# Two stacked transformer blocks on one core: gate products copied out of PSUM, modulation moved out of the second block's attention, raw context stream in its second layer

## The chip, the cores and the metric

The kernel runs on one core of a Trainium2 chip. The metric is the device time of one execution in microseconds (us), taken as the median of several runs. All arithmetic is float32; a matrix product is written as three matmuls on rounded halves (`hi`, `lo`) of both operands, which TensorE takes in its fp32r format.

## The reference

Two two-layer networks run one after the other on 256 latent tokens of width 1024.

`first_block`: per layer an RMS norm, three attention branches (neighbourhood, latent, windowed grouped-query), gates, an output projection, and a feed-forward net with a short convolution; a last RMS norm with `final_g`.

`second_block` takes that result as `x_lat`, with 256 context tokens `x_ctx` beside it. Cut to what the change touches:

```python
for l in range(DEPTH):
    last = l == DEPTH - 1
    m_lat = modulation(c, w_mod[l], b_mod[l])       # silu(c) @ w_mod + b: 6 vectors of 1024
    m_ctx = modulation(c_ctx, w_mod[l], b_mod[l])
    h_lat = modulate(rmsnorm_2(x_lat, norm1_g[l]), sh1, sc1)
    h_ctx = modulate(rmsnorm_2(x_ctx, norm1_g[l]), csh1, csc1)
    z_lat = h_lat @ w_in[l]                         # q, k, v, u, g
    z_ctx = h_ctx @ w_in[l][:, kv_lo:kv_hi] if last else h_ctx @ w_in[l]
    attn_lat = gqa_blocks(qh_l, concat(kh_c, kh_l), concat(vh_c, v_l))
    gm_lat = gelu(u_l) * spatial_mix(group_layernorm(gelu(g_l)))
    x_lat = x_lat + ga1 * (concat(attn_lat, gm_lat) @ w_out[l])
    x_lat = x_lat + ga2 * sqrelu_mlp(modulate(rmsnorm_2(x_lat, norm2_g[l]), sh2, sc2))
    # not last: the same two updates for x_ctx, with attention over the context alone
```

## The kernel before

Activations lie with features on partitions and tokens on the free axis: `xx` holds the latents in its columns 0 to 255 (`LAT`) and the context in 256 to 511 (`CTX`), as 8 tiles of 128 features. Weights come in pieces of 128 x 2048 by `load_w` (L161): one DMA on SyncE's queue into one of three `raw` buffers, then for each half a ScalarE copy to `hi` (L170) and a VectorE subtraction to `lo` (L172); five `hi` and five `lo` buffers exist. `pin[0]`, when set, keeps those `lo` subtractions behind a named VectorE instruction.

PSUM: four `acc` tiles for products, two `s` tiles for attention scores, one `pt` for transposes, one `o` for attention outputs and small sums. A matmul group waits until VectorE and ScalarE have read the tile that it takes over.

The instructions of each engine are put in order by the framework's scheduler from the order of the code, dependencies and priorities, so an edit can shift neighbours too. In the code, `weave(main, side, ratio)` runs `ratio` steps of a generator `side` per step of `main`.

Modulation: the 6 x 1024 modulation values of both layers and streams are dot products on VectorE (L280), in 192 steps; each step loads 128 x 512 of `w_mod` into one of two `mraw` buffers and makes two reductions of some 0.75 us (one in the last 64 of the steps). Steps 0 to 95 are layer 1, 96 to 191 layer 2. Every `load_w` ends with `tick()`, which adds the current rate to a counter and runs a step for each whole unit; `mod_until(n)` runs what is missing up to step n. `R1[layer]` holds the four rates of a layer of block 1 (start, attention and merge, up projection, down projection), `R2` the three of block 2 (preparation, attention, feed-forward).

Block 2, per layer, in the code's order: the projections of k, v and q (`z_lat`, `z_ctx`); q and k norms and rotation (`q_done`, `k_done`, collected in `prep`); the gate half of the gated unit (`g_half`, GELU and group statistics, `normalise`); then `attn()`, woven with `fill`: the `u` tiles of the gated unit (`gate_tile`, `twice_gelu`), their mixing matmuls (L1129), and the half of the output projection that needs them. The first `PRE[l]` steps of `fill` run ahead of attention. Then come the other half of the output projection, norm and feed-forward in four quarters `qq`, each four pieces up (FF1) and four down (FF2).

A stream can be multiplied in two ways. `mod_rows` makes the normed and modulated tile (L319, L321, L322) before the product. The other way, `raw_shift` and `raw_tile`, splits the unnormed tile times the scale, adds two columns for the shift (so 258 columns, `TE`), and the norm's row factor is applied to the product in `finish` (L898 to L902).

`twice_gelu` computes a GELU by tanh; its `x` is a PSUM tile `acc`, which is read by L1104, L1106 and L1108.

Of the kernel before, what the change touches and what calls it, by code (L numbers as in the profile page):

```python
# [3 lines left out]

# [1 line left out]

# [8 lines left out]
AF = mybir.ActivationFunctionType  # L15
# [6 lines left out]
T = 256  # L22
# [32 lines left out]

WV = (0.34, 1.48, 0.48)

R1 = ((0.0, 1.05, 0, 0.96), (0.23, 1.0, 0, 0.03))

R2 = (1.18, 1.45, 3.23)  # L60
SWAP16 = [i ^ 16 for i in range(32)]


# [12 lines left out]
def program(tc, A, out, stop=None):  # L76
# [10 lines left out]
    with top:  # L87
# [220 lines left out]
        def stream():  # L308

            return Parts([u8([P, 2, 4, TE], F32R) for _ in range(2)])  # L310
# [4 lines left out]
        def mod_rows(pool, bufs, row, a, sh, s, h):  # L315

            for k in range(KD):
                t = mk(pool, [P, T], tag="nt", bufs=bufs)
                V.scalar_tensor_tensor(t, xx[:, k, cut(s)], a[:, k, s : s + 1], row, op0=ALU.mult, op1=ALU.mult)  # L319
                hi, lo = h(k, slice(0, T))  # L320
                S.activation(hi, t, AF.Identity, bias=sh[:, k, s : s + 1])  # L321
                V.scalar_tensor_tensor(lo, t, sh[:, k, s : s + 1], hi.bitcast(F32), op0=ALU.add, op1=ALU.subtract)  # L322
# [8 lines left out]
        def raw_tile(a, s, e, k):  # L331

            return split(xx[:, k, cut(s)], *e(k, slice(0, T)), a[:, k, s : s + 1])
# [526 lines left out]
        def block2():  # L860
            with ExitStack() as st:
# [32 lines left out]
                def mm_x(ps, piece, x, n):  # L894
                    mm_w(ps[:, 0:n], piece, 0, KD, lambda k: x(k, slice(0, n)))
# [9 lines left out]
                for l in range(L):  # L905
# [53 lines left out]

                    def z_ctx(piece, z):  # L960
                        ps = acc()
                        mm_x(ps, piece, hc, T)
                        S.copy(z[:, CTX], ps[:, 0:T])

                    def k_done(kf):
                        rk = head_rms(kf, 4)
# [56 lines left out]
                    if l == 0:  # L1023
                        hc, e, al, wk = glob["start"]
                        row_l = frow[:, 1, :]
                    else:
                        hc = stream()
                        e, row_l, al = lat
                    zs = [tmp() for _ in range(6)]
                    hl = qtab = None  # L1030

# [23 lines left out]
                    else:  # L1055
# [4 lines left out]
                        wq = load_w(A["w_in2"][l, 0], 1024, 2048)  # L1060
                        done()
                        rows_of(rms_cols(tot[1], D), frow[:, 0, :])
                        mod_rows(kp, NT2, frow[:, 0, :], al, sh1, 1, hc)
                        q = u8p()
                        for i in range(2):
                            z_lat(wq[i], zs[2 + i])
# [25 lines left out]
                        next(second)  # L1092
                        next(prep, None)
                    normalise(0)
                    weave(second, prep, 1.0)
                    if l == 0:
                        for k in range(KD):
                            V.scalar_tensor_tensor(xx[:, k, LAT], xx[:, k, LAT], glob["fing"][:, k : k + 1], frow[:, 0, :], op0=ALU.mult, op1=ALU.mult)
                    gm = u8p()

                    def twice_gelu(dst, x, n):

                        th = tmp()[:, :n]
                        S.activation(th, x, AF.Square)  # L1104
                        V.tensor_scalar(th, th, 0.044715 * GC, GC, op0=ALU.mult, op1=ALU.add)
                        V.tensor_mul(th, th, x)  # L1106
                        S.activation(th, th, AF.Tanh)
                        V.scalar_tensor_tensor(dst, th, 1.0, x, op0=ALU.add, op1=ALU.mult)  # L1108

                    def mix_tasks():  # L1110

# [25 lines left out]

                        for g in range(4):
                            yield from gate_tile(g)
                            if g == 0:  # L1140
                                normalise(1)
                            if g:
                                mix(g - 1)
                        mix(3)
# [2 lines left out]
                    def attn():  # L1147
                        hold = {}

                        def front(j, side, b):  # L1150
# [12 lines left out]
                                src = [ps[:, i, :] for i in range(2)]  # L1163
                            s = sc[:, j, bb, :]
                            nm2 = small([P, 2], tag="nm2")
                            ins = V.tensor_mul(nm2, nm, s)
                            if last and (j, side, b) == (0, 0, 0):
                                pin[0] = ins
                            if side == 0:
                                p = [tmp(), tmp()]  # L1170
                            else:
# [38 lines left out]
                    fill = chain(mix_tasks(), out_half(1, gm, gate))  # L1210
                    mod_rate(R2[1])
                    ya = q
                    for _ in range(PRE[l]):
                        next(fill)
                    weave(attn(), fill, WV2[l])

                    def products(ap, x, cols_list, use, first=None):
# [38 lines left out]
                    for qq in range(4):  # L1256
# [19 lines left out]
                        if end and not last:  # L1276
                            mod_until(128)
                            al = scale_of(mods[l + 1], glob["par2"][:, l + 1, 0:8], 1)
                            lat = stream(), frow[:, 2, :], al
                            raw_shift(mods[l + 1][0], 0, lat[0])  # L1280
                            tot = [total_tile() for s in streams]

                        def down(mi, ps, cols):
                            m = 2 * c + mi
                            update(m, ps, 5, cols)
                            if end and last:
                                nc.sync.dma_start(out[:, m, :], xx[:, m, LAT])
                            elif end:
                                for s in range(cols.start // T, cols.stop // T):
                                    if s == 0:  # L1290
                                        raw_tile(al, 0, lat[0], m)
                                    add_square(tot[s], s, m)

                        for c in range(4):
# [138 lines left out]
```

## Time and profile before

| | us |
|---|---|
| median of 3 runs | 1785.15 (1783.11 to 1787.07) |
| the profiled execution, its own time | 1786.61 |
| its span, first to last instruction | 1784.8 |
| TensorE busy in the span | 1750.1 (98%) |
| VectorE busy | 1458.6 (82%) |
| ScalarE busy | 1017.7 (57%) |

Block 1 takes the span up to about 911 us, block 2's first layer from there to about 1471, its second layer the rest. Attention with its fill stands at about 976 to 1085 in the first layer, and at about 1518 to 1590 in the second. A busy share is a mean over stages, and matmuls overlap in the record, so a busy TensorE can still run below its pace; what it waits for is read stage by stage.

### The profile page before, as it was taken

To read this page: it belongs to the slowest core of one execution; us is meant where nothing else is said; L and a number is where in the kernel's file an instruction comes from. 1 tells how busy PE (TensorE), PEld (TensorE's weight loads), DVE (VectorE), ACT (ScalarE), POOL (GpSimd) and SP (SyncE) were. 2 spreads that over 40 slices of the span, in tenths; PEclk is the share of its full clock that TensorE was granted. 3 is DMA by queue.
4 is the path that set the end of the run, shared out by engine and by line. 5 is a ranking of instruction groups with operands and counts; after the bars stand their busy time and mean duration, and the time that the engine had idled before them with its cause. 6 is when DMAs were issued, how large, how long until landed. Compare 5 with 4: busy or idle time off the path is not lost.

```text
span 1784.8 us, 34096 instructions
## 1 busy us (share of the span) xinstructions
PE 1750.1 (98%) x13368; PEld 1673.0 (94%) x13368; DVE 1458.6 (82%) x3176; ACT 1017.7 (57%) x2007; POOL 83.5 (5%) x87
## 2 busy tenths in 40 slices
PE   8999999999999999999999999999999999899999
PEld 8999999999999999999999878989898989799999
DVE  8997899889898788988768878988675768877665
ACT  6866666665585666766554766424251536665453
POOL 0100210000010021000002000000000001000000
PEclk9999999999999999999999999999999999999999
DMA  7364664547645457454543212554545443225552
GB/s 286 127 220 173 208 231 168 187 165 247 212 160 196 171 184 248 168 188 155 189 164 108 90 49 80 179 182 164 178 156 181 145 151 118 94 67 197 187 189 95
DMA packets 69185, 297.11 MB, mean 166 GB/s; under 512 B 7840, under 2 KB 12448, under 8 KB 43424
## 3 DMA queue, kind: packets, MB, share of 16 engines
q1 hardware_dynamic: 68752, 294.67, 47.8%
q8 instruction: 105, 1.72, 0.4%
q14 instruction: 56, 0.46, 0.1%
q10 hardware_dynamic: 272, 0.26, 0.1%
HBM read 293.85 MB, written 1.05 MB: 165 GB/s over the span
## 4 chain that ended last, share of the span: by engine, by line
PE 80%; DVE 11%; ACT 5%; issue 2%; POOL 1%; DMA 0%; POOLq 0%; ACTq 0%; DVEq 0%
PE acc L180 23%; PE acc L182 23%; PE acc L181 23%; DVE lo L172 3%; PE s L180 2%; PE s L181 2%; PE s L182 2%; DVE u L205 1%; PE pt L411 1%; POOL rs_y L218 1%; ACT hi L170 1%; ACT p L386 1%; ACT p L397 1%; PE o L180 1%; DVE mjunk L280 1%
## 5 line engine op out<-in xcount | busy, mean ns | idle before, releaser
L180 PE MATMUL acc<-u,hi 128*128 128x256 f32 (+2 forms) x3604 | 1053.0, 293 | 8.0 <-DVE kf L1108 3.9
L181 PE MATMUL acc<-u,hi 128*128 128x256 f32 (+2 forms) x3604 | 1050.9, 292 | 1.0 <-DVE u L208 0.6
L182 PE MATMUL acc<-u,lo 128*128 128x256 f32 (+2 forms) x3604 | 1047.8, 291 | 1.2 <-DVE lo L172 1.0
L170 ACT CAST hi<-raw 128x1024 fp32r<-128x1024 f32 (+2 forms) x468 | 471.4, 1010 | 436.3 <-PE acc L181 381.0
L180 PEld LDWEIGHTS acc<-u,hi 128*128 128x128 f32 x3604 | 681.9, 189 | 24.9 <-DVE kf L1108 4.3
L181 PEld LDWEIGHTS acc<-u,hi 128*128 128x128 f32 x3604 | 682.8, 189 | 16.2 <-DVE u L208 1.9
L182 PEld LDWEIGHTS acc<-u,lo 128*128 128x128 f32 x3604 | 682.1, 189 | 15.1 <-DVE lo L172 2.1
L172 DVE TENSOR_TENSOR lo<-raw,hi 128x1024 fp32r<-128x1024 f32 (+2 forms) x468 | 551.2, 1184 | 101.7 <-ACT hi L170 95.8
L280 DVE CUSTOM_DVE_ANT_0 mjunk<-mraw,csil,mpart 128x512 bf16<-128x512 f32 x160 | 119.9, 749 | 9.0 <-DMA mraw<-in_w_mod 7.9
L280 DVE CUSTOM_DVE_ANT_0 mjunk<-mraw,csil,c_par 128x512 bf16<-128x512 f32 x160 | 120.2, 751 | 6.3 <-DMA mraw<-in_w_mod 5.2
L1189 DVE SCALAR_TENSOR_TENSOR xx<-acc,mods,xx 128x256 f32<-128x256 f32 x144 | 64.7, 479 | 57.7 <-PE acc L182 57.4
L218 POOL TENSOR_TENSOR rs_y<-rs_v,mhalf 128x2 f32<-128x2 f32 (+2 forms) x29 | 35.2, 1215 | 1080.3 <-DVE rs_v L216 1080.3
L204 ACT CAST u<-nt 128x256 fp32r<-128x256 f32 x146 | 57.2, 405 | 43.2 <-DVE nt L1272 35.0
L902 ACT ACTIVATE nt<-nt,shb 128x256 f32<-128x256 f32 x96 | 48.7, 510 | 57.3 <-DVE nt L901 57.3
L205 DVE TENSOR_TENSOR u<-nt,u 128x256 fp32r<-128x256 f32 x146 | 59.5, 421 | 17.2 <-ACT u L204 15.7
L182 PE MATMUL s<-u,lo 128*128 128x256 f32 x224 | 63.1, 282 | 0.5 <-DVE lo L172 0.5
L180 PE MATMUL s<-u,hi 128*128 128x256 f32 x224 | 62.9, 281 | 0.0
L181 PE MATMUL s<-u,hi 128*128 128x256 f32 x224 | 62.9, 281 | 0.0
L1272 DVE TENSOR_TENSOR nt<-nt 128x256 f32<-128x256 f32 x96 | 40.5, 423 | 19.4 <-ACT nt L902 13.3
L180 PE MATMUL acc<-hi,u 128*128 128x256 f32 (+1 forms) x168 | 48.5, 289 | 0.0
L182 PE MATMUL acc<-hi,u 128*128 128x256 f32 (+1 forms) x168 | 48.2, 287 | 0.0
L181 PE MATMUL acc<-lo,u 128*128 128x256 f32 (+1 forms) x168 | 48.1, 286 | 0.0
(249 smaller groups left out, 2059.2 us busy)
## 6 DMA issues: line engine op xcount, KB each, us to landing
raw<-in_w_ff SPq DMA_DIRECT2D x64, 1024.0 KB, 4.9
raw<-in_w_in SPq DMA_DIRECT2D x61, 1024.0 KB, 4.9
mraw<-in_w_mod SPq DMA_DIRECT2D x192, 256.0 KB, 3.4
raw<-in_w_up SPq DMA_DIRECT2D x44, 1024.0 KB, 4.9
raw<-in_w_down SPq DMA_DIRECT2D x32, 704.0 KB, 4.2
raw<-in_w_out SPq DMA_DIRECT2D x16, 1024.0 KB, 5.0
raw<-in_w_br SPq DMA_DIRECT2D x12, 1024.0 KB, 4.9
nbias<-in_na_bias SPq DMA_DIRECT2D x8, 384.0 KB, 3.0
```

The source lines that it names most:

```text
L170: S.copy(hi[:, : b - a], raw[:, a:b])
L172: last_lo[0] = V.tensor_sub(lo[:, : b - a], raw[:, a:b], hi[:, : b - a].bitcast(F32))
L180: PE.matmul(ps, a[0], b[0], start=start, stop=False)
L181: PE.matmul(ps, a[0], b[1], start=False, stop=False)
L182: return PE.matmul(ps, a[1], b[0], start=False, stop=stop)
L204: S.copy(hi, src)
L205: return V.tensor_sub(lo, src, hi.bitcast(F32))
L218: G.tensor_tensor(y, v, mhalf[:, :n] if len(shape)==2 else mhalf[:, :n].rearrange('p (a b) -> p a b', b=shape[2]), op=ALU.pow)
L280: V.tensor_tensor_reduce(out=junk, in0=w, in1=csil[:, i, half * 512 : half * 512 + 512], op0=ALU.mult, op1=ALU.add, scale=1.0, scalar=part ...
L902: S.activation(dst, dst, func, bias=b)
L1189: V.scalar_tensor_tensor(xx[:, m, cut(s)], ps[:, s * T - cols.start : s * T - cols.start + T], md[i][:, m, s : s + 1], xx[:, m, cut(s)], o ...
L1272: V.tensor_mul(r, r, r)
```

## The change

Eight edits:

1. `R1[1]` goes from (0.23, 1.0, 0, 0.03) to (0.23, 1.25, 0, 0.0), `R2` from (1.18, 1.45, 3.23) to (0, 0, 3.55): no modulation step is tied to a load of block 2's preparation and attention any more; more are in block 1's second attention and in the feed-forward of block 2's first layer.
2. `twice_gelu` copies `x` out of PSUM by ScalarE right behind the square, and the two VectorE instructions read the copy.
3. The context's k and v of the second layer are made from a raw stream. Its tiles are split at the end of the first layer's feed-forward; `mod_rows` for the context goes.
4. The scaling of the latents by `final_g` moves into the fill's third gate tile.
5. The second `normalise` moves from behind the first gate tile to behind the second.
6. The first `PRE[l]` steps of `fill` are woven with what is left of `prep`.
7. The pin on the first maximum of the second layer's attention goes.
8. An import (which moves every line number by one or more).

```diff
-R1 = ((0.0, 1.05, 0, 0.96), (0.23, 1.0, 0, 0.03))
+R1 = ((0.0, 1.05, 0, 0.96), (0.23, 1.25, 0, 0.0))
-R2 = (1.18, 1.45, 3.23)
+R2 = (0.0, 0.0, 3.55)
...
                     def z_ctx(piece, z):
                         ps = acc()
-                        mm_x(ps, piece, hc, T)
-                        S.copy(z[:, CTX], ps[:, 0:T])
+                        if last:
+                            mm_x(ps, piece, hc, TE)
+                            finish(ps, frow[:, 0, :], z[:, CTX], AF.Identity)
+                        else:
+                            mm_x(ps, piece, hc, T)
+                            S.copy(z[:, CTX], ps[:, 0:T])
...
-                        hc = stream()
-                        e, row_l, al = lat
+                        (e, hc), row_l, al = lat
...
                         rows_of(rms_cols(tot[1], D), frow[:, 0, :])
-                        mod_rows(kp, NT2, frow[:, 0, :], al, sh1, 1, hc)
...
                     normalise(0)
-                    weave(second, prep, 1.0)
-                    if l == 0:
-                        for k in range(KD):
-                            V.scalar_tensor_tensor(xx[:, k, LAT], xx[:, k, LAT], glob["fing"][:, k : k + 1], frow[:, 0, :], op0=ALU.mult, op1=ALU.mult)
...
                         S.activation(th, x, AF.Square)
+                        S.copy(dst, x)
                         V.tensor_scalar(th, th, 0.044715 * GC, GC, op0=ALU.mult, op1=ALU.add)
-                        V.tensor_mul(th, th, x)
+                        V.tensor_mul(th, th, dst)
                         S.activation(th, th, AF.Tanh)
-                        V.scalar_tensor_tensor(dst, th, 1.0, x, op0=ALU.add, op1=ALU.mult)
+                        V.scalar_tensor_tensor(dst, th, 1.0, dst, op0=ALU.add, op1=ALU.mult)
...
-                            if g == 0:
+                            if g == 1:
                                 normalise(1)
+                            if g == 2 and l == 0:
+                                for k in range(KD):
+                                    V.scalar_tensor_tensor(xx[:, k, LAT], xx[:, k, LAT], glob["fing"][:, k : k + 1], frow[:, 0, :], op0=ALU.mult, op1=ALU.mult)
...
-                            ins = V.tensor_mul(nm2, nm, s)
-                            if last and (j, side, b) == (0, 0, 0):
-                                pin[0] = ins
+                            V.tensor_mul(nm2, nm, s)
...
-                    for _ in range(PRE[l]):
-                        next(fill)
+                    weave(chain(second, islice(fill, PRE[l])), prep, 1.0)
                     weave(attn(), fill, WV2[l])
...
-                            lat = stream(), frow[:, 2, :], al
-                            raw_shift(mods[l + 1][0], 0, lat[0])
+                            lat = [stream(), stream()], frow[:, 2, :], al
+                            for s in streams:
+                                raw_shift(mods[l + 1][0], s, lat[0][s])
...
-                                    if s == 0:
-                                        raw_tile(al, 0, lat[0], m)
+                                    raw_tile(al, s, lat[0][s], m)
```

VectorE ahead of the first score maximum (L1158, now L1161) of block 2's first attention. `lo` is a weight's second half, `mjunk` a modulation reduction, BN rows are group statistics, `u` is the gate half being normalised. Before:

```order
L172 TENSOR_TENSOR lo_13464<-raw_13457,hi_13463 128x1024
L1008 BN_STATS bn_13103<-u_2241_12748 128x6
L1008 BN_STATS bn_13106<-u_2241_12748 128x6
L1009 BN_AGGR mv_12972<-bn_13103 128x2
L280 ISA mjunk_13470,mpart_13467<-mraw_13468,csil_106,c_par_65_267 128x512
L280 ISA mpart_13467 128x1
L1009 BN_AGGR mv_12972<-bn_13106 128x2
L172 TENSOR_TENSOR lo_13795<-raw_13792,hi_13794 128x1024
L216 TENSOR_SCALAR rs_v_13109<-mv_12972 128x8
L1158 TENSOR_REDUCE nm_13155<-s_13156 128x1
L1158 TENSOR_REDUCE nm_13155<-s_13161 128x1
```

The same place now:

```order
L173 TENSOR_TENSOR lo_13458<-raw_13451,hi_13457 128x1024
L1013 BN_STATS bn_13111<-u_2245_12755 128x6
L1013 BN_STATS bn_13114<-u_2245_12755 128x6
L1014 BN_AGGR mv_12972<-bn_13111 128x2
L1014 BN_AGGR mv_12972<-bn_13114 128x2
L173 TENSOR_TENSOR lo_13792<-raw_13789,hi_13791 128x1024
L217 TENSOR_SCALAR rs_v_13117<-mv_12972 128x8
L1026 TENSOR_SCALAR u_2245_12755<-u_2245_12755,mv_12972,rs_y_13119 128x128 x4
L1161 TENSOR_REDUCE nm_13147<-s_13148 128x1
L1161 TENSOR_REDUCE nm_13147<-s_13153 128x1
L1026 TENSOR_SCALAR u_2245_12755<-u_2245_12755,mv_12972,rs_y_13119 128x128
L1169 TENSOR_TENSOR nm_2311_13158<-nm_13147,sc_12260 128x2
```

The modulation reduction has gone from this stretch; four of the eight normalising instructions of the second half (L1026), which wait for GpSimd's `rs_y`, now stand ahead of the two maxima.

ScalarE at the first two gate tiles of the second layer; L1104 was the square and is now the copy, L1107 is the tanh, `hi` a weight's first half. Before:

```order
L1104 ACTIVATE kf_19286<-acc_19261 128x256
L204 CAST u_3392_18758<-kf_18626 128x256
L170 CAST hi_19795<-raw_19793 128x1024
L204 CAST u_3392_18758<-kf_18627 128x256
L1107 ACTIVATE kf_19286<-kf_19286 128x256
L1104 ACTIVATE kf_19322<-acc_19297 128x256
L1107 ACTIVATE kf_19322<-kf_19322 128x256
```

Now:

```order
L1103 ACTIVATE kf_19275<-acc_19250 128x256
L1104 COPY kf_19249<-acc_19250 128x256
L205 CAST u_3384_18750<-kf_18651 128x256
L171 CAST hi_19797<-raw_19795 128x1024
L1107 ACTIVATE kf_19275<-kf_19275 128x256
L1103 ACTIVATE kf_19317<-acc_19292 128x256
L1104 COPY kf_19291<-acc_19292 128x256
L1107 ACTIVATE kf_19317<-kf_19317 128x256
```

The last reader of each `acc` tile is now ScalarE's copy; the second tile's square and copy still stand behind the first tile's tanh, which waits for VectorE.

## Rows read from the trace of the kernel before

**Rows 1.** The page, busy time of each engine (us, share, instructions).
```profile
PE 1750.1 (98%) x13368; PEld 1673.0 (94%) x13368; DVE 1458.6 (82%) x3176; ACT 1017.7 (57%) x2007; POOL 83.5 (5%) x87
```

**Rows 2.** Busy time by stretch: us, PE PEld DVE ACT POOL, clock, DMA, GB/s.
```profile
484.00:560.00 76.00, 74.91 (x585) 71.62 (x584) 73.39 (x204) 58.89 (x144) 5.57 (x6) 1.00 0.49 170
560.00:715.00 155.00, 154.76 (x1254) 151.15 (x1253) 126.83 (x271) 94.42 (x186) 15.77 (x16) 1.00 0.58 201
976.00:1042.00 66.00, 58.78 (x389) 52.38 (x388) 52.82 (x123) 41.60 (x93) 1.64 (x1) 0.95 0.23 76
1113.00:1159.00 46.00, 45.92 (x359) 44.88 (x360) 45.85 (x117) 23.14 (x54) 0.00 (x0) 1.00 0.54 182
1159.00:1470.00 311.00, 311.00 (x1940) 279.84 (x1939) 230.64 (x514) 111.58 (x224) 0.00 (x0) 1.00 0.49 167
1515.00:1550.00 35.00, 27.92 (x171) 23.82 (x170) 29.68 (x77) 21.50 (x45) 3.08 (x3) 0.90 0.31 115
984.70:988.10 3.40, 3.21 (x9) 2.63 (x10) 3.00 (x13) 2.81 (x7) 0.00 (x0) 0.50 0.16 32
1524.00:1530.80 6.80, 5.24 (x18) 4.56 (x19) 5.27 (x9) 4.67 (x8) 0.00 (x0) 0.50 0.30 104
```

**Rows 3.** Modulation reductions alone (L280), VectorE busy by stretch.
```profile
930.00:976.00 46.00, 6.77 (x18) 1.00 0.27 93
1113.00:1159.00 46.00, 22.63 (x60) 1.00 0.54 182
```

**Rows 4.** TensorE's waits, 930 to 1113 us: releaser, us, times, longest.
```profile
PE s L180 <- ACT kf L386: 4.3, 2, 4.0
PE acc L180 <- DVE kf L1108: 1.8, 1, 1.8
PE o L935 <- DVE rs_v L216: 0.9, 1, 0.9
```

**Rows 5.** TensorE's waits, 1515 to 1600 us.
```profile
PE acc L180 <- DVE kf L1108: 2.1, 1, 2.1
PE acc L1129 <- DVE kf L1108: 2.0, 2, 1.5
PE o L181 <- DVE kf L205: 1.7, 3, 1.0
PE acc L180 <- ACT u L204: 1.3, 1, 1.3
```

**Rows 6.** Timeline, first layer's first scores: start us, us, engine, instruction.
```profile
973.51 1.65 DVE L1098 SCALAR_TENSOR_TENSOR xx<-xx,c_fing,frow 128x256 f32<-128x256 f32 x4
...
976.87 0.40 PE L182 MATMUL s<-kk,u 128*128 128x512 f32 x1
...
981.60 1.29 DVE L1158 TENSOR_REDUCE nm<-s 128x1 f32<-128x512 f32 x2
...
984.89 0.80 PE L180 MATMUL s<-kk,u 128*128 128x512 f32 x1 [4.01 <-ACT kf L386]
```

**Rows 7.** Timeline, one gate tile of the first layer.
```profile
1032.13 0.60 ACT L1104 ACTIVATE kf<-acc 128x512 f32<-128x512 f32 x1
...
1034.65 0.69 DVE L1108 SCALAR_TENSOR_TENSOR kf<-kf,acc 128x512 f32<-128x512 f32 x1 [0.70 <-ACT kf L1107]
...
1035.39 0.51 PE L180 MATMUL acc<-u,hi 128*128 128x512 f32 x1 [1.81 <-DVE kf L1108]
```

**Rows 8.** Groups by line and shape: count | busy us, mean ns | idle before.
```profile
L322 DVE SCALAR_TENSOR_TENSOR u<-nt,mods,u 128x256 fp32r<-128x256 f32 x16 | 6.9, 482 | 0.0
L319 DVE SCALAR_TENSOR_TENSOR nt<-xx,modA,frow 128x256 f32<-128x256 f32 x16 | 6.9, 481 | 1.1 <-ACT frow L228 1.1
...
L204 ACT CAST kf<-pt 128x512 fp32r<-128x512 f32 x24 | 14.0, 582 | 6.0 <-PE pt L411 5.8
L1106 DVE TENSOR_TENSOR kf<-kf,acc 128x512 f32<-128x512 f32 x4 | 2.7, 687 | 0.0
L1135 DVE SCALAR_TENSOR_TENSOR kf<-kf,kf 128x512 f32<-128x512 f32 x4 | 2.7, 685 | 0.1
```

More of the change, by code (lines that the diff above doesn't have):

```diff
@@ L3 @@
 from functools import partial
+from itertools import islice
 import numpy as np
```

## The prediction

> **What bounds the kernel now.** The first view is the page's busy time. TensorE is busy for 98% of the span, VectorE for 82%, ScalarE for 57% [rows 1]. That alone leaves little to gain: 34.7 us of the span without a running matmul. So the second view is busy time by stretch, and there the idle time is not spread. The first 66 us of block 2's first attention hold 7.2 us of it (66.00 less 58.78), and 35 us at the second layer's hold 7.1 us (35.00 less 27.92). The feed-forward behind the first has none in 311 us, and its first 46 us 0.08 us, with VectorE at 45.85 of 46 [rows 2]. A full VectorE is thus no cost by itself: it costs only where a matmul waits for its last word.
>
> The third view, TensorE's waits, says for what. In the first layer 4.3 us go to scores waiting for an exponential (`s` from `kf` L386) and 1.8 us to a product waiting until a gate tile has left PSUM (`acc` from L1108) [rows 4]; in the second, 2.1 and 2.0 us to the same gate tiles [rows 5]. After the long waits the granted clock falls to half (1.2 of 2.4 GHz). Two such windows are shown, 3.4 us and 6.8 us long at 0.50 [rows 2]; there are four in the two attentions, the other two of 3.4 us. A matmul then takes twice its time, so half of the busy time in a window is lost: 1.6 us in the first, 2.6 us in the long one, and 1.7 us in each of the others, where TensorE was busy throughout.
>
> **The change part by part.** The sum is made against the profiled execution's own 1786.6 us, 1.5 us above the median of the runs.
>
> *First scores of the first layer.* The scores are complete at 977.27 us (976.87 plus 0.40), but VectorE takes their maxima at 981.60, 4.3 us late, and the third score tile waits 4.01 us [rows 6]. VectorE is behind with modulation: nine reductions (18 instructions, each reduction having a small read beside it) take 6.77 us just before [rows 3]. In the changed order, between the latents' modulated rows and this maximum, I count 2 reductions where there were 11; nine times 0.75 us is 6.8 us less in front of the maximum, more than it was late. The scaling by `final_g` (1.65 us for four of its eight instructions in rows 6) does not leave the stretch, though the code moves it: the scheduler still puts it in front. What is late next: four normalising instructions now stand ahead of the maxima and wait for GpSimd. I leave 0.9 us for that. Of 4.0 + 1.6 = 5.6 us this gives back 4.7.
>
> *Gate products, first layer.* L1104 starts at 1032.13; the tile is let go when L1108 ends at 1035.34, and the next product, ready 1.81 us before 1035.39, starts then [rows 7]. With the copy, it is let go after the square and one ScalarE copy of 512 columns. The nearest row for that copy is a ScalarE cast of 512 columns out of PSUM, 582 ns [rows 8]: 1032.13 + 0.60 + 0.58 = 1033.31, before the product is ready at 1033.58. So the wait and its clock window go, 1.8 + 1.7 = 3.5 us; I take 3.2.
>
> *Gate products, second layer.* Waits of 2.1 and 2.0 us and 2.6 us of the long window, 6.7 us together. Here the second tile's square and copy stand on ScalarE behind the first tile's tanh, which waits for VectorE, so part of the second wait can stay. I take 5.2. Dropping the pin lets two weight subtractions run before the first maximum; VectorE has 3 us less to do there all the same (below).
>
> *The price of the copies.* Eight on ScalarE, at most 8 x 0.58 = 4.7 us, in stretches where it is busy 41.6 of 66 and 21.5 of 35 us [rows 2]. Behind each in its queue are exponentials and the casts of transposed scores, for which TensorE waits; the cost lies between 0 and 4.7 us, and I take 0.4, near the low end because ScalarE idles over a third of the time. [...] Here the ScalarE cast of 512 columns is shorter (582 ns) than VectorE's product of the same size (687 ns) [rows 8], so the row speaks for ScalarE. [...] The Trainium skill (Perfetto Trace Analysis, Optimizing Scalar/DVE Operations) also gives VectorE about 65 ns more per instruction on PSUM than on SBUF, which would make the 16 rerouted products 1.0 us cheaper; L1106 on PSUM takes 687 ns and L1135 on SBUF 685, so I count nothing.
>
> *Modulation moved.* By the order, 144 reductions stood before block 1's second up projection and 158 do now: 14 x 0.75 = 10.5 us more VectorE work in its attention and merge. In 484 to 560 VectorE has 2.6 us free, in 560 to 715 it has 28 us [rows 2]; one of the 14 falls in the first of these, the rest later. Below nothing it cannot be; above, all 10.5 us could come through; I take 0.5. Each pair of reductions brings a load on SyncE's queue in front of a weight load; three `raw` buffers cover it. In the first layer's feed-forward there are 160 reductions where there were 144, 12 us more, over 357 us in which VectorE has 80 us free: nothing, except in the first quarter, which is a rival below. Outside the two attentions, 0.9 us of waiting for VectorE in the preparation [rows 4] should go by about half: 0.5 us.
>
> *Raw context stream.* Gone: 16 VectorE instructions of 0.48 us [rows 8], 7.7 us, and 8 on ScalarE. Added: eight splits at the end of the feed-forward, about half of that, and two finishes. TensorE takes two columns more in 48 matmuls, 0.1 us. The work gone was beside running matmuls, so it gives nothing itself; it makes VectorE about 3 us earlier at the second layer's first maximum, which the gate term counts on.
>
> *New order.* The scheduler's order changes throughout both attentions. Some new gap will appear between transposes and outputs; I set 1.0 us, between the 1.7 us that such waits (`o` from `kf` L205) took in the second layer [rows 5] and none.
>
> Sum: -4.7 - 3.2 - 5.2 - 0.5 + 0.4 + 0.5 + 0.1 + 1.0 = -11.6. That is 1775.0 by the profiled execution and 1773.5 by the median; I predict 1774 us, with 1771 to 1777 as the likeliest case's own range.
>
> **The rivals.** *The attention's own chain takes over.* In the second layer's new order 36 matmuls of the fill stand between the first and second pair of scores, where 14 did; they are missing later, where a round of transpose, cast, subtraction and output stands bare. A bare step cost 0.6 us (1.7 us in 3) [rows 5]. Five more and one clock window of 2.6 us give back 5.6 us: 1780. For it: the waits were already there. Against: VectorE has less to do in the first layer's attention.
>
> *VectorE is late where it is full.* 22.5 us of reductions move into block 1's attention and the feed-forward. If they come through, block 1 loses 10.5 - 2.6 = 7.9 us. In the first quarter's FF1 the counter reaches 80 + 3 x 3.55 = 90.65, so `mod_until(96)` forces five or six steps, 9 us, ahead of the first update, while four `acc` tiles fill. With a clock window each that is 20 us: 1794. It decides from 11.6 us coming through. Against: the order has 37 reductions between the first square of FF1 and the first update, where it had 42, and TensorE waited 0.08 us there beside a full VectorE [rows 2].
>
> *It does not do what it says.* VectorE stays late at both first maxima through other work, and only the first layer's gate wait goes, with 1.5 us of new cost: 1785.
>
> *More comes back.* The output waits (1.7 us), the last wait of attention (1.3 us, `acc` from `u` L204) [rows 5] and its clock window (1.7 us) shrink too, as VectorE and ScalarE come earlier; two thirds of that with the 1.0 us of new gaps not arising: about 1770, with luck at other weight waits 1766.
>
> **How the numbers follow.** Chances: forecast 0.48, chain 0.22, full VectorE 0.08, no effect 0.10, more 0.12. A measurement here can tell about 0.2%, 3.6 us: faster means under 1781.6, slower over 1788.7. Faster: 0.48 + 0.12, and 0.21 of the chain and no-effect cases, 0.81. Slower: 0.08. The rest, 0.11, is the same. The range of 1766 to 1785 takes in all but the full-VectorE case and the edges.
>
> **What would show it.** Right: no wait of `s` for L386 over 1 us at the first scores; no `acc` wait for the last product of a gate tile; fewer half-clock windows in the attentions, two or fewer of the four; waits in block 1's second layer and in FF1 as before. Wrong: `acc` waits at the first down update or `lo` waits in block 1, or as much idle time in the attentions, named for `kf` L205 and `pt`.

## The result, and the profile after

After: 1768.79 us, median of 5 runs (1767.31 to 1770.5); before, also of 5 runs, 1785.15 (1783.11 to 1787.07). The ratio is 0.991, 95% interval 0.9896 to 0.9924: 16.4 us faster, where 11.2 were forecast, and inside the range of 1766 to 1785 us. The profiled execution took 1769.33 us with a span of 1767.5.

The page, busy time of each engine (us, share, instructions), answering to [rows 1]:

```profile
PE 1741.6 (99%) x13368; PEld 1666.7 (94%) x13368; DVE 1454.3 (82%) x3172; ACT 1018.2 (58%) x2019; POOL 84.9 (5%) x87
```

VectorE has as much to do as before. What changed is when.

Busy time by stretch, the columns as in [rows 2]: block 1's attention and merge (two rows), the first layer's attention, the first quarter of the feed-forward and the rest of it, the second layer's attention, and the one half-clock window that is left in the attentions.

```profile
484.00:560.00 76.00, 74.62 (x579) 71.15 (x578) 72.81 (x207) 59.67 (x143) 5.57 (x6) 1.00 0.48 160
560.00:715.00 155.00, 154.35 (x1250) 150.64 (x1249) 135.68 (x294) 93.04 (x183) 17.19 (x16) 1.00 0.62 215
975.00:1041.00 66.00, 65.53 (x444) 58.60 (x443) 51.47 (x110) 50.81 (x112) 1.32 (x1) 1.00 0.17 56
1110.00:1157.00 47.00, 47.00 (x326) 43.84 (x325) 44.35 (x111) 19.57 (x43) 0.00 (x0) 1.00 0.54 174
1157.00:1468.00 311.00, 310.13 (x1968) 279.77 (x1967) 240.36 (x550) 113.85 (x240) 1.56 (x2) 1.00 0.52 173
1505.00:1540.00 35.00, 30.94 (x211) 26.86 (x210) 31.31 (x70) 27.05 (x58) 0.33 (x1) 1.00 0.26 91
1571.60:1575.00 3.40, 3.40 (x17) 3.40 (x18) 2.17 (x6) 1.69 (x4) 0.00 (x0) 0.50 0.00 0
```

The first 66 us of the first layer's attention hold 0.47 us of idle TensorE where they held 7.2, with VectorE as busy as before (51.5 of 66 us against 52.8). The first 35 us at the second layer's hold 4.1 where they held 7.1.

TensorE's waits, 930 to 1113 us, answering to [rows 4] (releaser, us, times, longest):

```profile
PE s L181 <- ACT kf L387: 0.3, 1, 0.3
PE o L228 <- DVE diag L227: 0.2, 1, 0.2
```

The wait of 4.0 us at the first scores is 0.3 us, the gate tile's 1.8 us is gone, and so is the 0.9 us of `rs_v` in the preparation. The same view of 1515 to 1600 us, answering to [rows 5]:

```profile
PE pt L412 <- DVE kf L206: 1.5, 3, 0.7
PE s L181 <- ACT kf L387: 1.4, 1, 1.4
PE acc L181 <- ACT u L205: 1.3, 1, 1.3
PE o L182 <- DVE kf L206: 1.0, 3, 0.3
PE acc L181 <- DVE kf L1131: 0.4, 1, 0.4
```

No matmul waits for the end of a gate tile (now L1108, the same line). What is left is attention's own chain: scores, transposes, outputs, and its last wait.

Timeline of the first layer's first scores, answering to [rows 6] (start us, us, engine, instruction, idle before):

```profile
975.61 0.40 PE L183 MATMUL s<-kk,u 128*128 128x512 f32 x1
977.39 1.28 DVE L1161 TENSOR_REDUCE nm<-s 128x1 f32<-128x512 f32 x2
...
979.95 0.50 PE L181 MATMUL s<-kk,u 128*128 128x512 f32 x1 [0.33 <-ACT kf L387]
```

The maxima start 1.4 us after the scores are complete (976.01), where it was 4.3. One gate tile of the same layer, answering to [rows 7]:

```profile
1021.38 0.60 ACT L1103 ACTIVATE kf<-acc 128x512 f32<-128x512 f32 x1
...
1021.87 0.58 ACT L1104 COPY kf<-acc 128x512 f32<-128x512 f32 x1
...
1023.54 0.47 PE L181 MATMUL acc<-u,hi 128*128 128x512 f32 x1
```

The tile is let go at 1022.45, 1.07 us after the square began, where it was held for 3.21 us; the next product into an `acc` tile (1023.54) starts without a wait.

To see where the 16.4 us came from, the spans are cut at marks that every kernel has: the first score matmul of each layer's attention, the last one, and VectorE's first square of the feed-forward (FF1, L1272). Durations in us, from mark to mark, in one profiled execution of each kernel:

| stage | before | after | difference |
|---|---|---|---|
| start to first scores of layer 1 | 975.7 | 974.5 | -1.3 |
| layer 1: first scores to FF1 | 137.7 | 125.7 | -12.0 |
| FF1 to first scores of layer 2 | 405.2 | 407.1 | +1.9 |
| layer 2: first to last score | 55.3 | 49.3 | -6.0 |
| layer 2: last score to end of span | 211.0 | 211.0 | 0.0 |

### The profile page after: what moved, and what is told of

The parts are those of the page before. It is cut to its first block, busy times and chain, and to the rows that moved or that the text cites. A ratio compares the mean times of both kernels' runs of the same rounds, so it can differ in the third digit from the quotient of the medians.

```text
span 1767.5 us, 34134 instructions
## 1 busy us (share of the span) xinstructions
PE 1741.6 (99%) x13368; PEld 1666.7 (94%) x13368; DVE 1454.3 (82%) x3172; ACT 1018.2 (58%) x2019; POOL 84.9 (5%) x87
## 4 chain that ended last, share of the span: by engine, by line
PE 74%; DVE 15%; ACT 4%; DMA 3%; issue 3%; POOL 1%; DVEq 0%; POOLq 0%; ACTq 0%
PE acc L181 21%; PE acc L182 21%; PE acc L183 21%; DVE mjunk L281 3%; DVE lo L173 3%; DMA mraw<-in_w_mod 2%; PE s L181 2%; PE s L182 2%; PE s L183 2%; DVE u L206 2%; PE pt L412 2%; ACT hi L171 1%; PE o L181 1%; POOL rs_y L219 1%; ACT p L387 1%
## 5 line engine op out<-in xcount | busy, mean ns | idle before, releaser
L903 ACT ACTIVATE nt<-nt,shb 128x256 f32<-128x256 f32 x96 | 48.6, 509 | 70.6 <-DVE nt L902 70.5
L205 ACT CAST u<-nt 128x256 fp32r<-128x256 f32 x146 | 57.2, 405 | 53.0 <-DVE nt L1272 44.6
L206 DVE TENSOR_TENSOR u<-nt,u 128x256 fp32r<-128x256 f32 x146 | 59.3, 421 | 16.4 <-ACT u L205 14.8
L1272 DVE TENSOR_TENSOR nt<-nt 128x256 f32<-128x256 f32 x96 | 40.4, 422 | 16.8 <-ACT nt L903 10.8
```

Source lines behind the costliest of these rows:

```text
L205: S.copy(hi, src)
L206: return V.tensor_sub(lo, src, hi.bitcast(F32))
L903: S.activation(dst, dst, func, bias=b)
L1272: V.tensor_mul(r, r, r)
```

## The experiments

The forecast's theory gives each part its own wait: the rates the first scores, the copies the gate tiles of both layers, the raw context stream nothing of its own. The rivals are that the parts stand in for one another, since all of them change one thing, when VectorE is free; and that the new order carries part of the gain. Each part was taken back from after, then three were put alone into before, then the leftovers of the second layer were tried. A stage named below is one of the table. Two things limit the comparison. Before was timed again beside the later runs, at medians of 1785.18 to 1785.7 us, but after was not. And the ten kernels with the new rates are nearly one program up to the first scores, yet reach them at 974.0 to 975.8 us in their traces. So a difference of totals under some 2 us says little, and a stage says more than the total.

**The copies taken back.**

```diff
-S.copy(dst, x)
-V.tensor_mul(th, th, dst)
+V.tensor_mul(th, th, x)
-V.scalar_tensor_tensor(dst, th, 1.0, dst, ...)
+V.scalar_tensor_tensor(dst, th, 1.0, x, ...)
```

> The changed kernel with the copy out of PSUM taken back (the two VectorE instructions of a gate tile read the product in PSUM again); all else as changed. Theory 1, the prediction's steps: the gate products' waits for L1108 come back in both layers, 3.5 us in the first and 4 to 6.7 us in the second, with half-clock windows behind them: 1775 to 1779. Rival 1, VectorE's relief alone did it: with no modulation in the attention the gate tile's last VectorE read is early enough, so at most 2 us come back: 1769 to 1771. Rival 2, the gain is the scheduler's new order as a whole: the amount is not that of the gate waits, and waits of other names change with it.

Measured: 1771.43 us (1769.84 to 1775.59), ratio to before 0.9923 (0.9909 to 0.9937), 2.6 us over after, with overlapping ranges of runs. That is near rival 1 (1769 to 1771), by which VectorE's relief alone does most of it, and not theory 1's 1775 to 1779. TensorE's waits in the first layer, 930 to 1113 us:

```profile
PE acc L181 <- DVE kf L1107: 1.8, 1, 1.8
```

The wait of [rows 4] is back to the tenth of a microsecond, but no half-clock window follows it here, and the stage takes 128.05 us, 2.3 more than after. In the second layer only 0.5 us of waiting for the tile returns, and that stage is 0.7 us longer (50.0).

**The rates taken back.**

```diff
-R1 = ((0.0, 1.05, 0, 0.96), (0.23, 1.25, 0, 0.0))
+R1 = ((0.0, 1.05, 0, 0.96), (0.23, 1.0, 0, 0.03))
-R2 = (0.0, 0.0, 3.55)
+R2 = (1.18, 1.45, 3.23)
```

> The changed kernel with before's modulation rates (R1[1] = 0.23, 1.0, 0, 0.03; R2 = 1.18, 1.45, 3.23). Theory 1: VectorE is some 6.8 us later at the first scores of the first layer, the wait of the scores for the exponential returns (4 us and 1.6 us of half clock), while block 1's attention gets about 1 us shorter: 1773 to 1775. Rival 1, all of the gain beyond the copies is VectorE's relief over the whole attention of the first layer: 1776 to 1779. Rival 2, the weaving and not the rates closed the first wait: 1768 to 1770, and no wait of s for L387 over 1.5 us.

Measured: 1774.93 us (1773.22 to 1776.37), ratio 0.994 (0.9928 to 0.9953), 6.1 over after. Its waits, 930 to 1113 us, and behind them its half-clock window:

```profile
PE s L181 <- ACT kf L387: 4.9, 1, 4.9
PE o L936 <- DVE rs_v L217: 0.9, 1, 0.9
...
```

```profile
983.30:990.10 6.80, 5.29 (x19) 4.71 (x19) 6.36 (x18) 4.08 (x8) 0.00 (x0) 0.50 0.00 0
```

The first scores wait again, the preparation is 1.1 us longer, and the stage takes 133.5 us, 7.8 more than after: 4.9 of wait less the 0.3 left in after, and half of 5.29 = 2.6 for the window, together 7.2. The second layer is unchanged (49.27). So the rates are worth nothing there, and most of the gain in the first layer.

**The raw context stream taken back.**

```diff
...
-(e, hc), row_l, al = lat
+hc = stream()
+e, row_l, al = lat
...
+mod_rows(kp, NT2, frow[:, 0, :], al, sh1, 1, hc)
...
-raw_tile(al, s, lat[0][s], m)
+if s == 0:
+    raw_tile(al, 0, lat[0], m)
```

> The changed kernel with the second layer's context k and v made from a normed and modulated stream again. Theory 1: the work removed lay beside running matmuls; VectorE is about 3 us later at the second layer's first maximum, which the matmuls behind the first scores cover by half: 1769 to 1771. Rival, this edit carries the second layer's gain: 1773 to 1775.

Measured: 1772.49 us (1771.69 to 1773.3), ratio 0.9927 (0.9914 to 0.9941), 3.7 over after. Its waits from 1495 us, its half-clock window, and the timeline of VectorE ahead of that wait's end:

```profile
PE acc L183 <- DVE lo L173: 4.9, 1, 4.9
```

```profile
1511.90:1518.70 6.80, 4.16 (x13) 3.48 (x14) 6.80 (x14) 4.13 (x7) 0.00 (x0) 0.50 0.28 94
```

```profile
1511.24 0.68 DVE L1159 TENSOR_REDUCE nm<-s 128x1 f32<-128x512 f32 x1
1511.84 0.41 DVE L1106 SCALAR_TENSOR_TENSOR kf<-kf,kf 128x256 f32<-128x256 f32 x1
...
1512.24 1.11 DVE L1022 TENSOR_SCALAR u<-u,mv,rs_y 128x128 f32<-128x128 f32 x4
1513.27 2.35 DVE L173 TENSOR_TENSOR lo<-raw,hi 128x1024 fp32r<-128x1024 f32 x2
```

VectorE is late once more, and TensorE pays, though for a weight's `lo` and with the copies in place: a maximum, a gate product and the normalising rows all run before the subtraction. The first maximum itself is no later than in after (2.4 us behind its complete score tile against 2.3); it's the subtraction behind it that is late. The second layer's stage takes 53.6 us, 4.3 more than after. An edit that the forecast costed at nothing is the largest in this stage. The median lies between the two expectations.

**The new order taken back**: preparation not woven in, the scaling by `final_g` and the second `normalise` in their old places, the pin set again.

```diff
+weave(second, prep, 1.0)
...
-if g == 1:
+if g == 0:
     normalise(1)
...
+if last and (j, side, b) == (0, 0, 0):
+    pin[0] = ins
...
-weave(chain(second, islice(fill, PRE[l])), prep, 1.0)
+for _ in range(PRE[l]):
+    next(fill)
```

> The changed kernel with the preparation's weaving, the place of the final_g scaling, the place of the second normalise and the pin as before; rates, copy and raw context stream as changed. Theory 1: the scheduler had put the scaling ahead of the first maximum in either code, and the weaving moves few instructions, so 0 to 2 us come back: 1769 to 1771. Rival, the order of this stretch is what removed the wait at the first scores: 1773 to 1776 with a wait of s for L386 of 3 us or more.

Measured: 1767.64 us (1766.03 to 1771.06), ratio 0.9902 (0.9887 to 0.9917). The ranges of its runs and of after's overlap: no difference that can be told. In the second layer a 1.7 us wait for a `lo` stands where after waits 1.4 us at its scores, the stage takes 48.6 us, and no half-clock window is left in the attentions. Taken from after, the order carries none of the gain; put into before alone it was not run.

**The copies alone in before.**

```diff
+S.copy(dst, x)
-V.tensor_mul(th, th, x)
+V.tensor_mul(th, th, dst)
-V.scalar_tensor_tensor(dst, th, 1.0, x, ...)
+V.scalar_tensor_tensor(dst, th, 1.0, dst, ...)
```

> The kernel before with the copy of the gate product out of PSUM alone. Theory 1, the prediction's steps: the waits for L1108 and the half-clock windows behind them go in both layers, 3.2 + 5.2 us: 1776 to 1778. Theory 2, formed after the copy taken back from the changed kernel cost 2.6 us: a gate tile is held long only where VectorE is late, so copy and relief stand in for each other; with VectorE still late the copy alone must then give more than 2.6 us, 4 to 8 us: 1777 to 1781. Rival, VectorE's lateness turns each wait into another of the same length: 1783 to 1786.

Measured: 1777.5 us (1775.85 to 1778.25), ratio 0.9951 (0.994 to 0.9963), 8.0 under before. The waits from 1495 us:

```profile
PE acc L182 <- DVE lo L172: 4.9, 1, 4.9
...
```

The gate waits are gone in both layers. In the first it pays: 131.3 us, 6.3 less than before, though the 4.0 us at the first scores stay. In the second, 4.1 us of waiting for gate tiles [rows 5] have become 4.9 us for a `lo`, and the stage is only 1.6 us shorter (53.65). The total fits theories 1 and 2 alike, but the split is 6.3 and 1.6, not theory 1's 3.2 and 5.2, and in the second layer it's the rival that shows: one wait turned into another.

**The rates alone in before.** The edit is that of the rates taken back, the other way round.

```diff
-R1 = ((0.0, 1.05, 0, 0.96), (0.23, 1.0, 0, 0.03))
+R1 = ((0.0, 1.05, 0, 0.96), (0.23, 1.25, 0, 0.0))
-R2 = (1.18, 1.45, 3.23)
+R2 = (0.0, 0.0, 3.55)
```

> The kernel before with the changed modulation rates alone. Theory 1: the first scores' wait of 4 us and its clock window go, block 1 pays 0.5 to 1.5 us: 1779 to 1781. Theory 2 (copy and relief stand in for each other): the first layer's gate wait goes in part as well, 6 to 9 us: 1776 to 1779. Rival, the scaling by final_g and the normalising still stand ahead of the first maximum, so the wait stays: 1783 to 1786.

Measured: 1777.1 us (1775.64 to 1783.45), ratio 0.9959 (0.9945 to 0.9972), 8.4 under before. The waits of 930 to 1113 us:

```profile
PE acc L180 <- DVE kf L1108: 1.8, 1, 1.8
...
PE s L180 <- ACT kf L386: 0.3, 1, 0.3
```

The gate tile's wait is the same 1.8 us as in [rows 4], but the clock stays at full speed behind it, as in the first experiment. The stage takes 128.2 us, 9.5 less than before. So the 3.4 us window behind the gate tile, which the forecast charged to that tile, went with the rates. Theory 2 has the total right, but not its reason: the gate wait did not go in part. In the second layer all waits of [rows 5] are unchanged.

**Copies and raw stream both taken back.** The two edits above, together.

```diff
-S.copy(dst, x)
...
+mod_rows(kp, NT2, frow[:, 0, :], al, sh1, 1, hc)
```

> The changed kernel with both the copy and the raw context stream taken back. If the two edits are additive, the cost is 2.6 + 3.7 us: 1775. Theory 2, they stand in for each other in the second layer, where either one keeps the gate tiles from holding up the matmuls: the two waits for the gate tile's last read come back there, 4 us with 2.6 us of clock on top of the additive sum: 1778 to 1782. Rival, the first layer holds all of the copy's gain and the weight subtraction all of the raw stream's: 1774 to 1776 with waits for L1107 only in the first layer.

Measured: 1775.08 us (1774.51 to 1777.88), ratio 0.9943 (0.9931 to 0.9955), 6.3 over after, as much as the two alone (2.6 + 3.7). The waits from 1495 us:

```profile
PE acc L1126 <- DVE kf L1105: 2.0, 2, 1.5
PE acc L181 <- DVE kf L1105: 2.0, 1, 2.0
PE acc L183 <- DVE lo L173: 1.5, 1, 1.5
```

The gate waits of before are back, and a `lo` wait beside them, but the stage takes 54.1 us, only 0.5 over the raw stream's edit alone, and theory 2's 1778 to 1782 is refuted. The names of the waits change; what the stage pays hardly does.

**Raw stream alone in before.** The edit of the raw stream taken back, the other way round.

```diff
...
-hc = stream()
-e, row_l, al = lat
+(e, hc), row_l, al = lat
...
-mod_rows(kp, NT2, frow[:, 0, :], al, sh1, 1, hc)
...
-if s == 0:
-    raw_tile(al, 0, lat[0], m)
+raw_tile(al, s, lat[0][s], m)
```

> The kernel before with the raw context stream of the second layer alone. Theory 3, formed after the copy alone traded the second layer's gate waits for a wait of 5.0 us for a weight subtraction: VectorE's lag ahead of the second layer's attention is what TensorE pays for there, under whatever name, and this edit takes some 3 us off that lag; the gate waits of 4.1 us shrink by 2 to 4 us and their clock window with them: 1779 to 1782, all of it in the second layer. The prediction's step gave this edit nothing of its own: then 1784 to 1786. Rival: the copies are needed for any gain there: 1784 to 1786, the gate waits as before.

Measured: 1783.51 us (1779.19 to 1784.67, 12 runs), ratio 0.9986 (0.9977 to 0.9994): 2.2 under before, less than expected. The profiled execution took 1780.63, so its rows show more than the median does. VectorE's first maximum of the second layer, in before and then here, and the waits from 1495 us here:

```profile
1523.16 0.68 DVE L1158 TENSOR_REDUCE nm<-s 128x1 f32<-128x512 f32 x1
```

```profile
1518.57 0.68 DVE L1160 TENSOR_REDUCE nm<-s 128x1 f32<-128x512 f32 x1
```

```profile
PE acc L182 <- DVE lo L172: 2.0, 1, 2.0
PE o L181 <- DVE kf L205: 1.6, 3, 1.0
PE pt L411 <- DVE kf L205: 1.5, 3, 0.7
...
PE acc L1131 <- DVE kf L1110: 0.5, 1, 0.5
```

The score tile is complete at 1519.45 us in before and at 1518.07 here, so the maximum starts 3.7 us behind it there and 0.5 here; with the copies alone it is 3.7 again. That is the lag itself, 3.2 us shorter by this edit. Of the gate waits 0.5 us is left without any copy, and the stage takes 50.7 us, 4.6 less than before: idle time fell from 7.1 to 5.4 us, and the 6.8 us half-clock window (2.6 us lost) is gone. Of the other executions only the mean granted clock is known: seven of the twelve had 0.993 or 0.994 and took 1783.4 to 1784.7 us, five had 0.995 or 0.996 and took 1779.2 to 1783.2. So half-clock time gives much of the rest back; at which place isn't shown.

**One step of fill less ahead of the second layer's attention.**

```diff
-PRE = (1, 2)
+PRE = (1, 1)
```

> The changed kernel with one step of the fill instead of two ahead of the second layer's attention, so that a gate tile of 24 matmuls (2.8 us) is kept for the stretch at 1517 to 1532, where 5 us of waits stand in the changed kernel. Theory 2: the fill is short there, so 1 to 3 us come back: 1766 to 1768. Rival: the mixing matmuls wait for the later gate tile and the bare stretch only moves: 1769 to 1772.

Measured: 1773.93 us (1772.99 to 1775.05), ratio 0.9933 (0.992 to 0.9946): 5.1 over after, and the expectation missed. Its waits from 1495 us and its half-clock windows:

```profile
PE s L181 <- ACT kf L387: 2.6, 2, 1.8
PE acc L181 <- DVE kf L1131: 1.4, 1, 1.4
PE acc L181 <- ACT u L205: 1.3, 1, 1.3
```

```profile
1517.80:1524.60 6.80, 6.37 (x29) 5.71 (x28) 3.46 (x10) 5.58 (x13) 0.00 (x0) 0.50 0.48 182
1534.80:1541.60 6.80, 5.70 (x18) 4.49 (x19) 3.67 (x11) 3.56 (x8) 0.00 (x0) 0.50 0.01 1
```

Against after, `s` waits 1.2 us more and `acc` for L1131 1.0 more, and half of 6.37 + 5.70 is lost to the clock, 6.0 us, where after has no window in this stage. The stage takes 58.4 us, 9.1 more than after; the stage ahead of it, with a step less in it, gives part of that back. The expectation took the fill ahead of the scores as work that delays them; without it TensorE idles 1.7 us more in the stage and runs twice at half clock.

**One step more.**

```diff
-PRE = (1, 2)
+PRE = (1, 3)
```

> The changed kernel with three steps of the fill instead of two ahead of the second layer's attention; with one step it was 5 us slower. Theory 3: fill ahead of the first scores is what covers VectorE's lag, so one more gate tile ahead gives 0 to 2 us: 1767 to 1769. Rival: the fill is then missing in the rounds after, and bare output waits of 0.6 to 1.6 us come in its place: 1770 to 1773.

Measured: 1770.08 us (1767.72 to 1772.39), ratio 0.9914 (0.9901 to 0.9928), 1.3 over after, with overlapping ranges. The second layer's stage is 2.8 us shorter (46.5), and the stage ahead of it 3.4 us longer: the fill has only moved.

**The old order without the pin.** The experiment on the new order once more, without its pin.

```diff
-ins = V.tensor_mul(nm2, nm, s)
-if last and (j, side, b) == (0, 0, 0):
-    pin[0] = ins
+V.tensor_mul(nm2, nm, s)
```

> The changed kernel with the weaving, the final_g scaling and the second normalise as before, and without the pin. With the pin too as before the time was 1767.6 and a wait of 1.9 us for a weight subtraction stood in the second layer's attention. If the pin makes that wait, this gives 1765.5 to 1767; if the scheduler's order makes it, 1767 to 1769, and the pin is worth nothing.

Measured: 1768.34 us (1768.29 to 1770.83), ratio 0.9908 (0.9895 to 0.9921). Its runs lie among those of after and of the kernel with the pin: the pin is worth nothing that can be told. Its trace has no wait for `lo` any more, and 1.4 us at the scores as in after: one name for another once more.

**Fill spread over all of the second layer's attention**: 1.2 steps of fill for each step of attention.

```diff
-WV2 = (1.0, 1.55)
+WV2 = (1.0, 1.2)
```

> The changed kernel with 1.2 steps of fill per step of the second layer's attention instead of 1.55, so that one or two output tiles are left for its end, where TensorE waits 0.6 us for VectorE and 1.5 us for ScalarE's split of the last output. If these tiles then run beside that split, 1.5 to 2 us come back: 1766.5 to 1767.5. Rival: the rounds before miss them and wait as much more: 1768 to 1771.

Measured: 1765.59 us (1764.92 to 1766.22), ratio 0.9889 (0.9877 to 0.9902). All four runs lie under all five of after, by 3.2 us at the median: the best version here. Its waits from 1495 us, and busy time at the end of attention:

```profile
PE s L181 <- ACT kf L387: 1.4, 1, 1.4
PE o L182 <- DVE kf L206: 1.0, 3, 0.3
PE pt L412 <- DVE kf L206: 0.8, 2, 0.6
```

```profile
1560.00:1575.00 15.00, 14.99 (x122) 14.48 (x121) 10.29 (x21) 8.49 (x17) 0.00 (x0) 1.00 0.30 94
```

The last `acc` wait of 1.3 us is gone, one of three transposes waits no more, and no half-clock window is left in the attentions. The stage takes 45.1 us, 4.2 less than after. Part of that is only moved: from the last score to the end it takes 211.2 us, where the kernels with the old ratio and no half-clock window there take 209.6.

## Why the prediction was right, and where its sum was not

*What bounds.* Right. Idle TensorE stood in the two attentions, and VectorE's total said nothing: it fell by 4.3 us while the time fell by 16.4.

*First scores of the first layer, -4.7.* Right in mechanism, too small. The wait fell to 0.3 us where I had left 0.9, and the rates alone gave 9.5 us in this stage. Their gain counts the window behind the gate tile too (1.7 us, charged to the copies), so 4.0 - 0.3 + 1.6 + 1.7 = 7.0 us of it can be named, and for 2.5 the sum had no term. Taken from after, the rates cost 7.8.

*Gate products, first layer, -3.2.* The step was right: the copy took 590 ns (forecast 582) and the tile was free 1.1 us after its square began, as in the prediction's working. Its size depends on the other edit: 2.3 us when taken from after, 6.3 when put into before. The stage fell by 12.0 in all, and the raw stream and the order taken back leave it within 0.2 us, so rates and copies gave 12.0 together, not 9.5 + 6.3 = 15.8; the two terms were forecast at 7.9. Of the 3.8 us that they share, 1.6 is the clock (half-clock windows lost 3.3 us in before, 1.7 with the copies alone and none with the rates alone), and 0.6 idle time (8.08, 5.06 and 3.15 us, and 0.72 in after). For the other 1.6 no row has a name; that both cure one lag is the reading that fits, not a measurement.

*Gate products, second layer, -5.2.* This step failed as an attribution. I priced the waits by their names: 4.1 us of [rows 5] belong to gate tiles, so copies remove them. The copies alone turned them into a 4.9 us wait for a `lo` and gave 1.6 us; from after they take 0.7. The step on the raw context stream, "so it gives nothing itself", is the one that was wrong: in the traces the stream was worth 4.6 us of this stage put in and 4.3 taken out, and by the medians of the whole 2.2 and 3.7. I had seen that VectorE is 3 us earlier by it (3.2 by the traces), and had booked that to the copies. In this stage the two add up: 1.6 + 4.6 = 6.2 against 6.0 measured. That 5.2 came near 6.0 is luck: it was the right amount under the wrong edit.

*Price of the copies, +0.4.* No TensorE wait for ScalarE of more than 0.3 us stands in the first layer's attention after, so it was nearer nothing. The groups by line of after, 960 to 1110 us (count, busy us, mean ns, idle before):

```profile
L1108 DVE SCALAR_TENSOR_TENSOR kf<-kf,kf 128x512 f32<-128x512 f32 x4 | 2.8, 688 | 1.1 <-ACT kf L1107 1.1
L1106 DVE TENSOR_TENSOR kf<-kf,kf 128x512 f32<-128x512 f32 x4 | 2.7, 686 | 0.1
...
L1104 ACT COPY kf<-acc 128x512 f32<-128x512 f32 x4 | 2.4, 590 | 0.0
```

VectorE's product takes 686 ns from SBUF where it took 687 from PSUM [rows 8], so nothing was gained by the reroute, as counted. No run has a VectorE copy of such a tile out of PSUM to set beside ScalarE's 590 ns; VectorE's one-operand read of that size, the maximum L1161, takes 685 ns. And ScalarE is the engine that wasn't late.

*Modulation moved, +0.5, and preparation, -0.5.* Some of the moved work did come through: block 1's second up projection begins at 728.0 to 728.8 us in the four traces with the old rates and at 729.2 to 730.9 in the ten with the new, and block 1's last update at 905.0 and 906.0 on their means, 1.0 us later where 0.5 was set. From there to the first scores it is 69.9 us in before, 68.8 in after and with the rates alone, and 69.9 with the rates taken back: the preparation gave 1.1 us, by the rates. The rival of a full VectorE is refuted: FF1's first stretch ran 47.00 us of 47 with 44.35 us of VectorE. Its count of reductions there (42 and 37) isn't that of the traces, which have 34 between the first square and the first update in either kernel.

*New order, +1.0.* Gaps of this kind are there: `pt` 1.5 and `o` 1.0 us in the second layer, and 1.4 us at its scores. As an edit the order cost and gave nothing that could be told, and these gaps are not its own: the kernel with the old order and no pin has the same three, and with the pin 0.8, 0.7 and 0.3 us beside the 1.7 for a `lo`. Not foreseen was 0.8 us of a new wait at `k_done` (`o` for `kf` L976, ending at 1490.65 us), part of the +1.9 us between the attentions. It belongs to the raw stream: it stands in the kernel with the stream alone (L975 there) and in no kernel without it.

*The rivals.* Of what the forecast named as signs, all came as it said: 0.3 us at the first scores, no gate wait, one half-clock window of four. In time the result is that of "more comes back" (1766 to 1770), but not by its reason: the output waits fell only from 1.7 to 1.0 us, and the last wait of attention stayed, with its half-clock window, and went only in the last experiment.

*Open.* The same last wait of attention (`acc` for `u` L205, 1.3 us) is followed by a half-clock window in after, and not in the kernel without the copies, nor in the others with one edit taken back. So each of them is 1.4 us shorter than after's trace from the last score on (209.6 against 211.0), whatever its edit cost. No run here tells what decides it. About 1.3 us of the first layer's 12.0 are named by nothing: idle time fell by 7.4 us in the stage (8.1 to 0.7), and two half-clock windows had cost 3.3.

## What to carry to other kernels

When a late engine is paid for in several waits, price the engine's lag, not the waits by name: here clearing one made the next reader of that engine pay, until work left the engine ahead of that point. Copy a PSUM tile out on an idle engine when a long chain of readers holds it, and take away work ahead of a first use even if it runs beside matmuls. Then spread the filling work until the last bare step of the chain has some beside it.

## What the runs showed of the hardware

A half-clock window took 1.6 to 3.2 us of matmul time (half of 3.21 and of 6.37), as much as many of the waits, but the length of the wait ahead of it did not decide it. Behind the same 1.8 us at a gate tile the granted clock was 0.50 for 3.4 us in before, and 1.00 both in before with the new rates and in after without the copies. The rows of these three, in that order:

```profile
1035.90:1039.30 3.40, 3.40 (x10) 2.65 (x10) 2.36 (x5) 1.94 (x5) 0.00 (x0) 0.50 0.00 0
```

```profile
1027.30:1037.30 10.00, 9.96 (x47) 7.91 (x48) 7.92 (x16) 6.22 (x15) 0.00 (x0) 1.00 0.07 26
```

```profile
1026.90:1036.90 10.00, 10.00 (x47) 7.95 (x48) 7.99 (x16) 6.24 (x14) 0.00 (x0) 1.00 0.08 26
```

ScalarE's copy of 512 columns out of PSUM took 590 ns, less than a VectorE product of that size (686 ns) or its maximum over one (685 ns).
